# A smaller descriptor scratch, and one more place for weight chunks, in an mLSTM, convolution, attention and expert layer

## The chip, the cores and the metric

The kernel runs on one core of a Trainium2 chip. The metric is the device time of one execution in microseconds; of the kernel before there are three runs and one profiled execution.

## What is computed

One layer of an encoder over 512 tokens of width 1024, in float32. A mixer adds three gated branches (a bidirectional mLSTM with 4 heads, a depthwise convolution of width 31, an attention with 8 heads and low-rank queries and keys), projected by `w_out`, to the input. Then each of 16 experts picks its 64 best tokens and adds a SwiGLU layer of them:

```
x   = x + W_out( sum_b sigmoid(G_b xn) * Branch_b(xn) ),  xn = RMSNorm(x)
aff = softmax(RMSNorm(x) @ w_router);  gate, idx = top_k(aff.T, 64)
h   = silu(xg @ w_e_gate) * (xg @ w_e_up)          # xg: the picked tokens, 64 x 1024 per expert
x   = x + scatter_add(idx, (h @ w_e_down) * gate)  # w_e_*: 16 x 1024 x 1536, 302 MB in all
```

## The kernel before

**The mixer** runs first. Projections are done in three float32r products per pair of tiles (high and low halves, split by ScalarE and VectorE at L166 and L167). At its start stands a stage for the mLSTM's gates: `agr`, the gains of its norm (128 x 512 floats, 256 kB), is asked for by GpSimd (POOL) at L582, `gf` is copied from `gall` by VectorE at L585, ScalarE takes `ab` from it in three steps (L587 to L589), GpSimd fills `zero`, `bc` and `mr` with zeros (L593 to L597), and VectorE scans (L600, L606). The scans end in `mrh`, which TensorE needs at L671. `agr` is first read by the norm of the first head (L734). All these tiles lie where tiles of the attention lay, so that their first writers wait for the attention's last products (`poa`, L560).

**The output projection** `w_out` runs in four column blocks n of 256, each over four token tiles (`pso`, L177 to L179 called at L964 ff.). The weights of blocks 2 and 3 are loaded in four pieces each (`woraw`, two buffers, L820) and split into `wo`. The router is computed between.

**The experts** go in pairs. Their weights come in chunks of 128 x 3072 floats (12 kB in each partition, 1536 kB in all, L892). A pair has 24: eight for each expert's gate and up products (`pg`, `pu`, `pm`, L1145), eight for the down products of both (`pd`, L1217). SP issues all chunk loads. Places for chunks lie in four rings, opened as memory comes free: the first while `w_out` is running, the second when one of its weight tiles is closed, the third and fourth when the mixer's pools are closed. Two chunks are loaded ahead into tiles whose own use comes later, `work` and `acc`. Places are taken in turn (`SLOTS`); a chunk that has been used calls for the next load (`used`), unless it lay in one of those two tiles.

```
RINGS = (8, 2, 1, 1)
ORDER = (0, 1, 2, 3, 4, 5, 6, 8, 9, 10, 7, 11, 12, 13)
AHEAD = (2, 5, RINGS[0])
...
        if n + 2 < NQ:
            for k in range(0, KT, 2):
                load_wo(n + 2, k, 2)
            for c in range(AHEAD[n], AHEAD[n + 1]):
                load(ORDER[c])
...
    def used(n):
        del chunks[n]
        if n not in own and nload[0] < NCH:
            load(nload[0])
            nload[0] += 1
```

The order of instructions on an engine or queue is not quite that of the program: a planner may put a later one first when it expects the earlier one to wait. Pools are stacked from two sides of each partition's memory; 16 kB of it are kept as scratch for the descriptors of transfers that GpSimd issues.

Of the kernel before, what the change touches and what calls it, by code (L numbers as in the profile page):

```python
# [36 lines left out]
CH = 2 * FF  # L37
# [11 lines left out]
MAGIC = float(0x5F3759DF)  # L49
LN_AT = 4  # L50
WARM = 10
RINGS = (8, 2, 1, 1)


ORDER = (0, 1, 2, 3, 4, 5, 6, 8, 9, 10, 7, 11, 12, 13)
SLOTS = [r for r, n in enumerate(RINGS) for _ in range(n)]
AHEAD = (2, 5, RINGS[0])
CONSTS = (
# [28 lines left out]
def hybrid_mlstm_conv_mla_ec_encoder_kernel(  # L87
    ctx: ExitStack, tc: tile.TileContext, a: dict, out: bass.AP, dbg=None
):
    nc = tc.nc  # L90
    PE, V, A, G, SY = nc.tensor, nc.vector, nc.scalar, nc.gpsimd, nc.sync
# [487 lines left out]
    mrl = gk.tile([NR, S], F32R, name="mrl")  # L579
    cols = gk.tile([P, 2, NT, NR], F32, name="cols")  # L580
    agr = gk.tile([P, HA, P], F32, name="agr")
    G.dma_start(agr, a["a_norm_g"])  # L582
    w1 = pools.open("w1")
    gf = w1.tile([NR, S], F32, name="gf")
    V.tensor_copy(gf, gall[64 : 64 + NR, :])  # L585
# [270 lines left out]
    )  # L856
    rings = [pools.open("ring1", RINGS[0])]
    seq = [0]
# [22 lines left out]
    def load(n, place=None):  # L881
        c = place
        if c is None:
            c = rings[SLOTS[seq[0] % len(SLOTS)]].tile(
                [P, CH], F32, tag="chunk", name="chunk"
            )
            seq[0] += 1
        src = source(n)
        w = src.shape[1]
        step = CH // 3 if n == NCH - 1 else w  # L890
        for c0 in range(0, w, step):
            SY.dma_start(c[:, c0 : c0 + step], src[:, c0 : c0 + step])  # L892
        chunks[n] = c

    for n in range(AHEAD[0]):
        load(ORDER[n])
    wrg = rt.tile([P, KT, NE], F32, name="wrg")
# [63 lines left out]
    for n in range(NQ):  # L961
# [19 lines left out]
# [5 lines that stand above are left out]
        if n == NQ - 2:  # L986
            pools.close("wo0")
            rings.append(pools.open("ring2", RINGS[1]))
            for c in range(RINGS[0], RINGS[0] + RINGS[1]):
                load(ORDER[c])  # L990

# [8 lines left out]

    rings.append(pools.open("ring4", RINGS[3], side="right"))
    rings.insert(2, pools.open("ring3", RINGS[2], side="right"))
# [5 lines left out]
    work = ex2.tile([P, CH], F32, name="work")  # L1008
# [4 lines left out]


    accf = acc.rearrange("p t d -> p (t d)")
    own = {7: work, 13: accf[:, :CH]}
    for n in ORDER[RINGS[0] + RINGS[1] :]:
        load(n, own.get(n))
    nload = [len(ORDER)]

# [429 lines left out]
def _build(nc, arrays, dbg=None):  # L1450
    args = {
        k: nc.dram_tensor(
            f"in_{k}_dram", v.shape, mybir.dt.from_np(v.dtype), kind="ExternalInput"
        ).ap()
        for k, v in arrays.items()
    }
    out = nc.dram_tensor("out_0_dram", (S, D), F32, kind="ExternalOutput").ap()
    with tile.TileContext(nc) as tc:
        hybrid_mlstm_conv_mla_ec_encoder_kernel(
            tc, args, out, dbg(nc) if dbg else None  # L1460
        )
# [13 lines left out]
```

## Time and profile before

| | |
|---|---|
| median of 3 runs | 1282.27 us (1282.19 to 1282.41) |
| profiled execution | 1281.83 us |
| its span in the trace | 1280.1 us |
| mean granted TensorE clock | 0.995 |
| TensorE busy | 1233.7 us, 96% |
| VectorE, ScalarE, GpSimd busy | 596.9, 287.0, 23.7 us |
| moved by transfers | 351.05 MB, 274 GB/s on average |

The profiled execution is 1.73 us longer than its span, for what lies around it. Engines are PE (TensorE), PEld (its weight loads), DVE (VectorE), ACT (ScalarE), POOL (GpSimd) and SP; a q behind the name is the engine's sequencer or queue. The page cuts the span into 40 slices of 32 us.

### The profile page before, as it was taken

The page shows a single profiled execution, that of the slowest core. Times are in us where ns is not written, and L with a number is a line of the kernel's source. Part 1 is how long each engine was busy: PE and PEld are TensorE (multiplying, and loading weights), DVE is VectorE, ACT ScalarE, POOL GpSimd, SP SyncE. Part 2 cuts the span into 40 slices and gives each one's busy share as a digit, 9 for nine tenths or more (in the row PEclk, how much of TensorE's full clock was granted, in tenths as well). Part 3 has the DMA queues.
Part 4 walks back from the last instruction along what each step waited for, and adds up shares of the span by engine and source line. Part 5 has one row for each costly group of instructions (what it writes and reads, how often), then busy time and mean ns, then how long its engine had stood idle before and what let it go on. Part 6 is the DMA issues. An engine that isn't in the chain of part 4 may idle for free.

```text
span 1280.1 us, 15572 instructions
## 1 busy us (share of the span) xinstructions
PE 1233.7 (96%) x6224; PEld 735.6 (57%) x6224; DVE 596.9 (47%) x1438; ACT 287.0 (22%) x560; POOL 23.7 (2%) x56
## 2 busy tenths in 40 slices
PE   6999999999999999999999999999999999988997
PEld 6997777768878888994344353443433433423432
DVE  7379999999874655344321323213131231131122
ACT  5354444445333443221100000001000000010010
POOL 2000000001000000000000000000000000000000
PEclk9999999999999999999999999999999999999999
DMA  6231211112123244588999999999999999999996
GB/s 247 81 93 29 77 54 51 50 48 76 50 67 99 83 129 149 206 351 334 392 380 427 425 425 425 425 426 425 424 425 426 426 424 424 425 425 426 426 423 273
DMA packets 43496, 351.05 MB, mean 274 GB/s; under 512 B 4960, under 2 KB 5856, under 8 KB 18208
## 3 DMA queue, kind: packets, MB, share of 16 engines
q1 hardware_dynamic: 42768, 348.75, 67.7%
q8 instruction: 49, 0.80, 0.3%
q10 hardware_dynamic: 576, 1.05, 0.2%
q0 software_dynamic: 80, 0.26, 0.1%
q14 instruction: 23, 0.19, 0.0%
HBM read 347.94 MB, written 2.10 MB: 273 GB/s over the span
## 4 chain that ended last, share of the span: by engine, by line
PE 75%; DMA 19%; DVE 4%; ACT 1%; issue 1%; DVEq 0%; ACTq 0%; SPq 0%
DMA chunk<-in_w_gu_dram 9%; DMA chunk<-in_w_dn_dram 9%; PE pd L1217 8%; PE pg L1145 6%; PE pu L1145 6%; PE pm L1145 5%; PE psg L178 3%; PE psg L179 3%; PE psg L177 3%; PE px L1056 3%; PE psz L177 3%; PE psz L178 2%; PE psz L179 2%; PE psy L178 2%; PE psy L179 2%; PE psy L177 2%
## 5 line engine op out<-in xcount | busy, mean ns | idle before, releaser
L1217 PE MATMUL pd<-chunk,work 128*64 128x512 f32 x672 | 161.3, 607 | 5.7 <-DMA chunk<-in_w_dn_dram 5.7
L1145 PE MATMUL pg<-chunk,xg 128*64 128x512 f32 x504 | 148.3, 600 | 6.0 <-DMA chunk<-in_w_gu_dram 5.9
L1145 PE MATMUL pu<-chunk,xg 128*64 128x512 f32 x504 | 145.6, 593 | 0.0
L1145 PE MATMUL pm<-chunk,xg 128*64 128x512 f32 x504 | 137.8, 593 | 0.0
L1157 DVE SCALAR_TENSOR_TENSOR work<-pu,rsl,work 128x512 f32<-128x512 f32 x16 | 12.0, 751 | 211.0 <-PE pu L1145 211.0
L1217 PEld LDWEIGHTS pd<-chunk,work 128*64 128x64 f32 x672 | 48.3, 139 | 98.1 <-issue 88.1
L167 DVE TENSOR_TENSOR wlo<-wraw,whi 128x1024 fp32r<-128x1024 f32 x56 | 68.4, 1224 | 40.6 <-ACT whi L166 40.2
L167 DVE TENSOR_TENSOR yhl<-pd,yhl 128x512 fp32r<-128x512 f32 x18 | 12.4, 692 | 160.2 <-ACT yhl L166 160.2
L754 DVE SCALAR_TENSOR_TENSOR cacc<-upad,hwb,cacc 128x512 f32<-128x512 f32 x120 | 86.8, 743 | 0.1
L1156 ACT ACTIVATE work<-pg,rsl 128x512 f32<-128x512 f32 x16 | 11.0, 687 | 337.9 <-PE pg L1145 328.7
L166 ACT CAST whi<-wraw 128x1024 fp32r<-128x1024 f32 x56 | 58.8, 1052 | 112.7 <-PE psg L178 65.8
L1145 PEld LDWEIGHTS pu<-chunk,xg 128*64 128x64 f32 x504 | 40.1, 137 | 70.8 <-issue 70.8
L1145 PEld LDWEIGHTS pm<-chunk,xg 128*64 128x64 f32 x504 | 38.7, 137 | 71.6 <-issue 71.6
L177 PE MATMUL psg<-xh,whi 128*128 128x512 f32 x192 | 76.3, 397 | 2.5 <-ACT whi L166 2.5
L1145 PEld LDWEIGHTS pg<-chunk,xg 128*64 128x64 f32 x504 | 37.1, 136 | 72.0 <-issue 56.5
L178 PE MATMUL psg<-xl,whi 128*128 128x512 f32 x192 | 76.8, 400 | 0.0
L179 PE MATMUL psg<-xh,wlo 128*128 128x512 f32 x192 | 75.9, 395 | 0.0
L178 PE MATMUL psz<-xl,whi 128*128 128x512 f32 x160 | 64.7, 404 | 0.0
L179 PE MATMUL psz<-xh,wlo 128*128 128x512 f32 x160 | 64.6, 404 | 0.0
L177 PE MATMUL psz<-xh,whi 128*128 128x512 f32 x160 | 64.5, 403 | 0.0
L1036 DVE SCALAR_TENSOR_TENSOR yhl<-pb,affr,before 128x512 fp32r<-128x512 f32 x64 | 47.8, 746 | 31.1 <-PE pb L1033 31.1
L166 ACT CAST yhl<-pd 128x512 fp32r<-128x512 f32 x18 | 10.5, 586 | 217.0 <-PE pd L1217 192.4
(374 smaller groups left out, 2091.6 us busy)
## 6 DMA issues: line engine op xcount, KB each, us to landing
chunk<-in_w_gu_dram SPq DMA_DIRECT2D x118, 1536.0 KB, 26.5
chunk<-in_w_dn_dram SPq DMA_DIRECT2D x60, 1536.0 KB, 29.4
wraw<-in_w_z_dram SPq DMA_DIRECT2D x44, 512.0 KB, 3.5
chunk<-in_w_ga_dram SPq DMA_DIRECT2D x8, 1024.0 KB, 24.1
chunk<-in_w_dl_dram SPq DMA_DIRECT2D x3, 1536.0 KB, 23.9
mxt<-in_x_dram SPq DMA_DIRECT2D x8, 512.0 KB, 5.0
chunk<-in_w_gb_dram SPq DMA_DIRECT2D x2, 1536.0 KB, 21.6
nraw<-in_w_v_dram SPq DMA_DIRECT2D x2, 1024.0 KB, 5.4
```

The lines of the kernel that those rows point to most:

```text
L166: A.copy(hi, src)
L167: eng.tensor_sub(lo, src, hi.bitcast(F32))
L177: PE.matmul(ps, lh, rh, start=i == 0, stop=False)
L178: PE.matmul(ps, lh, rl, start=False, stop=False)
L179: PE.matmul(ps, ll, rh, start=False, stop=i == n - 1)
L754: V.scalar_tensor_tensor(cacc[:, i], u, w, cacc[:, i], op0=ALU.mult, op1=ALU.add)
L1036: V.scalar_tensor_tensor(rjunk, pb, aff[:, t, e : e + 1], before[:, (NT - 1 - t) * P : (NT - 1 - t) * P + S], op0=ALU.subtract, op1=ALU.is_gt,
L1056: PE.matmul(px[:, kk], x1[:, t, k * P : (k + 1) * P], flat[:, t], start=t == 0, stop=t == NT - 1,)
L1145: last = PE.matmul(ps[hf * 64 : hf * 64 + 64, :], xs, w[:, o : o + S], start=k == 0, stop=k == KT - 1,)
L1156: A.activation(hb[:, 0], pg, AF.Silu, scale=r)
L1157: V.scalar_tensor_tensor(hb[:, 0], pu, gr, hb[:, 0], op0=ALU.mult, op1=ALU.mult)
L1217: last = PE.matmul(pd[i * 64 : i * 64 + 64, :], hT[i][:, rt], chunks[ns[i]][:, r * S : (r + 1) * S], start=rt == 0, stop=rt == 11,)
```

## The change

The descriptor scratch is 1 kB instead of 16, and the first ring has nine places instead of eight. The chunks loaded ahead of the first use are fifteen instead of fourteen: chunk 11 comes ahead of chunk 7, and `acc` takes chunk 14 instead of 13. The transfer of `agr`, the only one that GpSimd issues, is issued by ScalarE.

```
-RINGS = (8, 2, 1, 1)
-ORDER = (0, 1, 2, 3, 4, 5, 6, 8, 9, 10, 7, 11, 12, 13)
+RINGS = (9, 2, 1, 1)
+ORDER = (0, 1, 2, 3, 4, 5, 6, 8, 9, 10, 11, 7, 12, 13, 14)
...
-    G.dma_start(agr, a["a_norm_g"])
+    A.dma_start(agr, a["a_norm_g"])
...
-    own = {7: work, 13: accf[:, :CH]}
+    own = {7: work, 14: accf[:, :CH]}
...
-    nc = _bacc.Bacc("TRN2", target_bir_lowering=False, num_devices=1)
+    nc = _bacc.Bacc("TRN2", target_bir_lowering=False, num_devices=1, dynamic_dma_scratch_size=1024)
```

## Rows read from the trace of the kernel before

**Rows 1.** The page: an engine's busy time, and transfer rate in 40 slices.

```profile
PE 1233.7 (96%) x6224; PEld 735.6 (57%) x6224; DVE 596.9 (47%) x1438; ACT 287.0 (22%) x560; POOL 23.7 (2%) x56
...
GB/s 247 81 93 29 77 54 51 50 48 76 50 67 99 83 129 149 206 351 334 392 380 427 425 425 425 425 426 425 424 425 426 426 424 424 425 425 426 426 423 273
```

**Rows 2.** Busy time by stretch; the last columns are granted clock, transfer share, GB/s.

```profile
595.00:680.00 85.00, 85.00 (x424) 34.67 (x422) 22.05 (x59) 6.89 (x11) 0.00 (x0) 1.00 0.95 386
...
680.00:760.00 80.00, 79.30 (x392) 32.91 (x390) 19.85 (x48) 5.24 (x9) 0.00 (x0) 1.00 1.01 425
```

**Rows 3.** The chain that ended last, 1040 to 1180 us (start, length, what).

```profile
1134.05 29.47 DMA chunk<-in_w_dn_dram
1163.57 5.36 PE pd L1217 x22
```

**Rows 4.** Waits of TensorE from 860 to 1170 us (total, times, longest).

```profile
PE pg L1145 <- DMA chunk<-in_w_gu_dram: 5.9, 7, 0.9
PE pd L1217 <- DMA chunk<-in_w_dn_dram: 5.7, 6, 2.0
```

**Rows 5.** Busy time by stretches of 5 us, columns as in rows 2.

```profile
555.00:560.00 5.00, 5.00 (x45) 5.00 (x45) 2.42 (x7) 1.29 (x4) 0.00 (x0) 1.00 0.30 104
575.00:580.00 5.00, 4.54 (x36) 3.91 (x34) 4.02 (x23) 1.86 (x7) 0.00 (x0) 1.00 0.27 111
...
665.00:670.00 5.00, 5.00 (x22) 2.31 (x24) 2.48 (x4) 0.00 (x0) 0.00 (x0) 1.00 0.64 270
```

**Rows 6.** SP's queue from 538 to 598 us (start, length, line, transfer, count).

```profile
539.92 1.83 SPq L820 DMA_DIRECT2D woraw<-in_w_out_dram  x2
541.81 0.43 SPq L892 DMA_DIRECT2D chunk<-in_w_gu_dram  x1
557.36 1.83 SPq L820 DMA_DIRECT2D woraw<-in_w_out_dram  x2
559.25 7.04 SPq L892 DMA_DIRECT2D chunk<-in_w_gu_dram  x4
579.58 0.33 SPq L892 DMA_DIRECT2D work<-in_w_gu_dram  x1
...
596.37 0.33 SPq L892 DMA_DIRECT2D chunk<-in_w_gu_dram  x1
```

**Rows 7.** What SP's queue waited for, 600 to 690 us.

```profile
SPq L892 <- PE pm L1145: 52.0, 15, 7.9
SPq L892 <- PE pd L1217: 27.7, 6, 10.9
```

**Rows 8.** Timeline of ScalarE, VectorE and GpSimd from 268 to 272 us.

```profile
268.28 1.09 ACT L655 ACTIVATE ao<-psz 128x512 f32<-128x512 f32 x2 [2.99 <-PE poa L560]
...
268.86 0.74 POOL L582 DMA_DIRECT2D agr<-in_a_norm_g_dram  x1 [217.54 <-PE poa L560]
269.01 2.35 DVE L585 COPY gf<-gall 36x512 f32<-36x512 f32 x1
...
270.53 0.55 POOL L597 MEMSET mr<- 36x512 f32 x1
...
271.39 0.63 ACT L587 ACTIVATE ab<-gf 36x512 f32<-36x512 f32 x1 [1.51 <-DVE gf L585]
```

**Rows 9.** Timeline of VectorE: the next operation on `gf`.

```profile
272.66 0.41 DVE L590 TENSOR_SCALAR gf<-gf 36x512 f32<-36x512 f32 x1
```

**Rows 10.** Line 1275, the output's transfers: ns shortest, median, longest.

```profile
L1275 ACTq DMA_DIRECT2D out_dram<-acc x4: 338/338/377, 1270.5 to 1276.8; - x4
```

**Rows 11.** Waits of TensorE from 250 to 595 us.

```profile
PE psg L177 <- ACT whi L166: 2.5, 1, 2.5
...
PE pr L671 <- ACT mrh L169: 0.5, 1, 0.5
```

**Rows 12.** Timeline: last split of `w_out`'s last block, and that block's first product.

```profile
564.73 0.69 DVE L167 TENSOR_TENSOR wo<-woraw,wo 128x512 fp32r<-128x512 f32 x1 [0.42 <-ACT wo L166]
...
567.02 0.36 PE L177 MATMUL pso<-wo,mgh 128*128 128x256 f32 x1
```

## The prediction

> **What bounds the kernel now.** I read the page first, then the busy time by stretch, the chain that ended last, the waits of TensorE and the order of SP's queue. The page shows TensorE busy nearly throughout and the transfer rate rising to 425 GB/s from the middle on [rows 1]. The question is which of the two sets the end. By stretch, the transfers run at 386 GB/s on average from 595 to 680 us and at 425 from 680 on [rows 2], and the page holds that rate until the last slice [rows 1]. So from about 680 us the stream of weight chunks has no gap left. The chain shows what the end hangs on: its last transfer is a w_dn chunk that lands at 1134.05 + 29.47 = 1163.5 us, and the down products start on it at once [rows 3]; what follows in the chain is TensorE's own work. Before that, TensorE waits for chunks 13 times, 5.9 + 5.7 = 11.6 us in all, between 860 and 1170 us [rows 4]. Hence the end is: the landing of that chunk, plus work that comes after it. A stream that is earlier by d moves the end by d, as long as d stays under those 11.6 us.
>
> What sets the stream's place in time? Before 680 us it has holes. Three carry the argument: 555 to 560 us at 104 GB/s, 575 to 580 us at 111, 665 to 670 us at 270 [rows 5]. Against 425 they are 5 x 321/425 = 3.8 us, 5 x 314/425 = 3.7 us and 5 x 155/425 = 1.8 us of idle transfer. The first two lie where SP has nothing it may issue: between the single chunk at 541.81 and the pair of w_out pieces at 557.36, and between the four chunks from 559.25 and `work` at 579.58 [rows 6]. The third is of another kind. From 600 to 690 us SP's loads wait for places: 52.0 us for `pm` and 27.7 us for `pd` products that still read the old chunk [rows 7]. The stream after the last hole is therefore anchored to TensorE: one load for each chunk that TensorE gives up, started when it gives it up.
>
> **The ring, part by part.** A chunk is 128 x 12 kB = 1.573 MB, at 425 GB/s [rows 2] 3.70 us. With the ninth place in the first ring fifteen chunks are asked for before TensorE uses any, instead of fourteen. The load that follows the use of chunk m is then one chunk further on in the weights than today, for every m from 14 on (from 0 to 12 as well; at m = 13 it is two, since the chunk held in `acc` is now 14 and not 13). TensorE gives places up at the same times, because until about 860 us it waits for no chunk. So each transfer slot behind the hole at 665 us carries the next chunk, and each chunk lands one slot, 3.70 us, earlier. The bytes are the same; what pays is that the extra chunk goes through in a hole.
>
> Where it goes through: its load stands among those of the stage that issues at 541.81 and 559.25 [rows 6]. Behind either it meets a hole of 3.8 or 3.7 us [rows 5], as long as itself. Should it be pushed behind 579.58, the holes between 595 and 680 us still take it: 85 x (425 - 386)/425 = 7.8 us of idle transfer [rows 2]. If none took it, it would cost nothing and bring nothing. Bounds: 0 and 3.70 us gained; I take 3.70, since a hole of that length stands beside either place in the queue.
>
> The new order (11 ahead of 7, 14 in `acc`) and the renumbered places issue nothing more. Chunk 7 goes to `work`, still at 579.58, behind TensorE's last `pso`; it lands some 7 us later and is the eighth to be used, while TensorE's first use is about 596 us, when the next load goes out [rows 6]. That cover is over 10 us, and if it were gone the cost would be one chunk, 3.70 us, in a stretch where the 11.6 us of later waits would take it up. The ninth place costs no wait that I can find: its ring opens on the side and at the height where only tiles of earlier branches have lain. The smaller scratch has no time of its own: after the change no transfer is issued from POOL.
>
> **The move of `agr`.** Today POOL issues it at 268.86 us for 0.74 us and then does its three memsets, the last ending at 270.53 + 0.55 = 271.08 [rows 8]. Over just that time VectorE's copy `gf` of 36 x 512 takes 2.35 us and ends at 271.36, 0.28 us behind the last memset [rows 8]; an operation on the same tile from SBUF to SBUF takes 0.41 [rows 9]. So the copy stands still while POOL works. Without the 0.74 us in front, the memsets can end 0.74 us earlier, and the copy with them. Behind it ScalarE has been idle 1.51 us for `gf` [rows 8], TensorE then waits 2.5 us for a cast that stands behind ScalarE's steps on it, and 0.5 us for `mrh`, the end of VectorE's scans [rows 11]. TensorE is short of work there, so I pass the 0.74 us on to the end in full. Bounds: nothing, if the copy is slow for a reason of its own, and 2.35 - 0.41 = 1.94 us, if the memsets leave the stretch too.
>
> The Trainium skill, page "SBUF — State Buffer", section "SBUF: two separate sides", states that VectorE and GpSimd share a pair of ports that the first to start holds for its whole instruction while the other waits. By that rule the 0.74 us is real and the sum is 4.44; this trace agrees, with the copy's end 0.28 us behind POOL's. The Trainium skill, page "DMA: Bandwidth & Descriptors", section "Issuing engines are not separate DMA queues", says that the choice of the issuing engine saves only the time to initiate the transfer, which speaks against a gain here. By that the sum is 3.70; no run yet shows it.
>
> ScalarE now holds the transfer. The nearest row is its issue of the output, 0.338 us [rows 10]. It must wait, as POOL did, until the attention's last products have ended; queued behind it are the `ao` activations, the casts of `oT` and the steps on `gf`. ScalarE was idle for the end of those same products, and idle again for the 1.51 us before `ab` [rows 8], so I take nothing. Without that cover it would be 0.34 us, by POOL's own row 0.74.
>
> **Sum.** Profiled execution: 1281.83 - 3.70 - 0.74 = 1277.39 us. It stands 0.44 under the median of the runs, so 1277.8 for the median. With both bounds of `agr`: 1282.27 - 3.70 - 1.94 = 1276.6, and 1282.27 - 3.70 + 0.34 = 1278.9.
>
> **Rivals.**
> Only the place pays: the copy `gf` is slow for itself, or the time won there is lost in planning. For it: that the copy waits is inferred from ends that follow one another, from one row. 1282.27 - 3.70 = 1278.6 us.
>
> The place is filled and nothing moves: the load ends up where the stream had no hole, or TensorE's work behind 1163.5 us turns out to be held by something other than the chunk. For it: TensorE is 96% busy [rows 1], so little slack is left. Against it: 11.6 us of waits for chunks in front of that point [rows 4]. Time: only `agr`, 1281.5 us.
>
> Slower: the extra load goes in front of w_out. The order of SP's queue is planned, and today one chunk already goes between the two pairs of w_out pieces [rows 6]. The last piece is split by 564.73 + 0.69 = 565.4 us, and the product that starts on w_out's last quarter runs from 567.02 [rows 12]; its later rows of weights leave some 3.5 us of slack. The second pair goes out when the first has been split. If n chunks came ahead of the first pair at 539.92, the pieces would be 3.70 n later: two give a stall of 7.4 - 3.5 = 3.9 us, under the gain of 4.4; three give 7.6 us, and the sum 1282.27 - 4.44 + 7.6 = 1285.4; four (all of that group) 11.3 us, 1289.1. It decides from three on. Against it: the kernel writes all loads behind the pieces.
>
> A larger gain: besides all this the memsets clear the copy's way, or TensorE's 2.5 us idle closes further: 1276 us or below.
>
> **How the numbers follow.** Place and `agr` together 0.57, the place alone 0.16, nothing moves 0.11, slower 0.10, larger gain 0.06. The likeliest gives 1277.8, in its own range 1276.6 to 1278.9. Upwards I reach to the case in which nothing moves: 1276.3 to 1281.9. A measurement here can tell about 0.2%, 2.56 us, from no change. The first, second and last case are faster by more than that, 0.79, of which I take off 0.02 for holes that are only partly filled: 0.77; within it 0.13; slower 0.10.
>
> **What would show it.** Right: four chunks from the group behind 541.81 instead of three; the hole at 555 or 575 us nearly gone; the hole at 665 us still there at the same length; TensorE's waits for chunks down from 11.6 to about 8 us; `gf` at some 1.6 us and ending near 270.6. Wrong: a `pso` product that waits for `wo`, ScalarE held in front of 268.28 us, a hole at 665 us that has grown by a chunk, or waits for chunks that have not shrunk.

## The result, and the profile after

The changed kernel takes 1276.03 us (median of 6 runs, 1275.37 to 1279.43), the kernel before 1282.34 in the same set (6 runs, 1282.19 to 1285.32): the ratio is 0.995, with a 95% interval of 0.994 to 0.9961. It is 6.3 us faster. The forecast was 1277.8, and its range began at 1276.3, so the time fell 0.27 us below the range: the direction was right and the gain too small.

The profiled execution of this set is the slowest of its six, 1279.43 us with a span of 1277.7. A second set of runs of the same kernel (experiment e0 below) has its median, 1275.82, as its profiled execution, with a span of 1274.1. Both are read here.

The page of the first, TensorE's line, to [rows 1]:

```profile
PE 1230.5 (96%) x6224; PEld 734.1 (57%) x6224; DVE 596.2 (47%) x1438; ACT 287.1 (22%) x560; POOL 23.2 (2%) x55
```

Busy time by stretch of the changed kernel, to [rows 2, 5] and with their columns:

```profile
595.00:680.00 85.00, 85.00 (x421) 35.24 (x418) 20.81 (x52) 6.90 (x11) 0.00 (x0) 1.00 0.96 388
665.00:670.00 5.00, 5.00 (x26) 1.65 (x24) 0.80 (x2) 0.00 (x0) 0.00 (x0) 1.00 0.70 256
680.00:760.00 80.00, 79.30 (x392) 32.21 (x391) 19.46 (x47) 5.24 (x9) 0.00 (x0) 1.00 1.01 426
```

SP's queue of the changed kernel up to 600 us, to [rows 6]:

```profile
539.46 0.42 SPq L892 DMA_DIRECT2D chunk<-in_w_gu_dram  x1
555.02 1.83 SPq L820 DMA_DIRECT2D woraw<-in_w_out_dram  x2
556.90 7.04 SPq L892 DMA_DIRECT2D chunk<-in_w_gu_dram  x5
577.22 0.33 SPq L892 DMA_DIRECT2D work<-in_w_gu_dram  x1
...
594.01 0.33 SPq L892 DMA_DIRECT2D chunk<-in_w_gu_dram  x1
596.59 2.90 SPq L892 DMA_DIRECT2D chunk<-in_w_dn_dram  x2
```

The extra chunk stands in the second group, which has five chunks instead of four. Since the mixer ends 2.4 us earlier here, the two holes ahead of 595 us stand some 2.4 us earlier too. Busy time in stretches of 10 us around each of them, first in the kernel before, then in the changed one:

```profile
552.40:562.40 10.00, 10.00 (x89) 10.00 (x88) 3.79 (x14) 3.98 (x12) 0.00 (x0) 1.00 0.60 212
574.60:584.60 10.00, 9.48 (x62) 7.89 (x61) 7.65 (x44) 3.10 (x11) 0.00 (x0) 1.00 0.57 214
```

```profile
550.00:560.00 10.00, 10.00 (x88) 10.00 (x88) 3.80 (x14) 3.87 (x12) 0.00 (x0) 1.00 0.62 226
572.20:582.20 10.00, 9.48 (x63) 7.93 (x61) 7.65 (x44) 3.11 (x11) 0.00 (x0) 1.00 0.91 354
```

The first hole is as empty as before. The second carries (354 - 214) x 10 = 1.40 MB more (1.55 in e0, with 369 GB/s), against 1.573 MB of a chunk: that is where the extra chunk went through. The hole at 665 us is still there. At 594 us one chunk of `w_gu` is left to ask for instead of two, and then `w_dn` begins: each load behind TensorE's use of a chunk now brings the next one.

Timeline of ScalarE's queue, VectorE and GpSimd in the changed kernel, to [rows 8]:

```profile
266.60 0.39 ACTq L582 DMA_DIRECT2D agr<-in_a_norm_g_dram  x1
266.68 0.52 POOL L593 MEMSET zero<- 36x512 f32 x1 [214.97 <-PE poa L560]
267.14 0.52 POOL L595 MEMSET bc<- 36x512 f32 x1
267.32 0.62 DVE L585 COPY gf<-gall 36x512 f32<-36x512 f32 x1
267.61 0.81 POOL L597 MEMSET mr<- 36x512 f32 x1
268.01 0.62 ACT L587 ACTIVATE ab<-gf 36x512 f32<-36x512 f32 x1
```

The copy `gf` takes 0.62 us instead of 2.35 and no longer stands behind the last memset: it ends at 267.94, 0.28 us behind the second, and the third, with 0.81 instead of 0.55 us, is the one that gets longer. What follows in TensorE (its waits from 250 to 595 us, to [rows 11]):

```profile
PE pr L671 <- ACT mrh L169: 1.2, 1, 1.2
...
PE pc L616 <- DVE al L604: 1.1, 1, 1.1
```

The single wait of 2.5 us is gone, and so is the short one of 0.5; two of 1.2 and 1.1 stand in their place. In the kernel before, TensorE's clock fell behind that wait. Its busy time by stretches of 1 us shows it in the granted clock, the third column from the end:

```profile
278.00:279.00 1.00, 1.00 (x4) 0.81 (x3) 0.99 (x2) 0.99 (x2) 0.00 (x0) 0.50 0.00 0
279.00:280.00 1.00, 1.00 (x3) 0.80 (x3) 0.97 (x2) 1.00 (x2) 0.00 (x0) 0.50 0.00 0
280.00:281.00 1.00, 1.00 (x4) 0.74 (x3) 1.00 (x2) 0.29 (x1) 0.00 (x0) 0.50 0.00 0
```

At 0.50 (1.2 GHz) eight products follow one another every 0.43 us from 277.50 on, where the same products stand 0.23 us apart at 2.4 GHz: that is 8 x 0.2 = 1.6 us lost. In the changed kernel the clock is 1.00 throughout that stretch.

The end of the chain, to [rows 3], in the first profile and in that of e0:

```profile
1130.07 29.47 DMA chunk<-in_w_dn_dram
1159.58 7.06 PE pd L1217 x22
```

```profile
1128.10 29.48 DMA chunk<-in_w_dn_dram
1157.62 5.36 PE pd L1217 x22
```

The chunk lands at 1157.58 us in e0, 5.9 earlier than before. In the first profile it lands 2.0 us later than in e0, and the 22 products behind it take 7.06 us instead of 5.36, since the clock falls behind the wait for that chunk (0.83 from 1160 to 1170 us). These two things are its 3.6 us over e0, and the same program gave both. In e0 the clock falls as well, but one chunk earlier (0.85 from 1150 to 1160 us): the products there end later, and the wait for the last chunk is 0.6 us instead of 2.0. TensorE's waits for chunks, from 850 to 1180 us, in the two, to [rows 4]:

```profile
PE pd L1217 <- DMA chunk<-in_w_dn_dram: 6.3, 5, 2.0
PE pg L1145 <- DMA chunk<-in_w_gu_dram: 6.0, 7, 0.9
```

```profile
PE pg L1145 <- DMA chunk<-in_w_gu_dram: 6.1, 8, 0.9
...
PE pd L1217 <- DMA chunk<-in_w_dn_dram: 2.9, 4, 1.0
```

### The profile page after: what moved, and what is told of

The parts are those of the page before. It is cut to its first block, busy times and chain, and to the rows that moved or that the text cites. A ratio compares the mean times of both kernels' runs of the same rounds, so it can differ in the third digit from the quotient of the medians.

```text
span 1277.7 us, 15571 instructions
## 1 busy us (share of the span) xinstructions
PE 1230.5 (96%) x6224; PEld 734.1 (57%) x6224; DVE 596.2 (47%) x1438; ACT 287.1 (22%) x560; POOL 23.2 (2%) x55
## 4 chain that ended last, share of the span: by engine, by line
PE 82%; DMA 12%; DVE 4%; ACT 1%; issue 1%; SPq 0%; DVEq 0%; ACTq 0%
PE pd L1217 11%; DMA chunk<-in_w_dn_dram 7%; PE pg L1145 7%; PE pu L1145 6%; PE pm L1145 6%; DMA chunk<-in_w_gu_dram 5%; PE px L1056 4%; PE psg L179 3%; PE psg L177 3%; PE psg L178 3%; PE psz L178 3%; PE psz L179 3%; PE psz L177 3%; PE pxs L1271 2%; PE psy L177 2%; PE psy L178 2%
```

## The experiments

The kernel before was timed beside each set: 1283.35 us for e0 to e3, 1282.73 for e4 to e7, 1283.56 for e8 and e9, one run of 1282.79 for e10 and e11. The table splits each profiled execution at the mixer's end, taken as the start of the last `pso` product; the rest runs from there to the end of the span. No experiment leaves any of the computation out.

| | median us (range) | ratio, 95% interval | profiled | mixer's end | rest |
|---|---|---|---|---|---|
| before | 1282.34 | | 1281.83 | 579.27 | 700.8 |
| after | 1276.03 (1275.37 to 1279.43) | 0.995 (0.994 to 0.9961) | 1279.43 | 576.91 | 700.8 |
| e0 | 1275.82 (1275.34 to 1276.77) | 0.9941 (0.9929 to 0.9953) | 1275.82 | 576.85 | 697.3 |
| e1 | 1288.70 (1288.11 to 1288.82) | 1.0039 (1.0026 to 1.0052) | 1288.82 | 584.62 | 702.5 |
| e2 | 1279.33 (1278.95 to 1281.36) | 0.997 (0.9959 to 0.9981) | 1279.33 | 576.28 | 701.3 |
| e3 | 1277.97 (1276.83 to 1279.05) | 0.9956 (0.9944 to 0.9968) | 1276.84 | 577.98 | 697.1 |
| e4 | 1276.05 (1275.11 to 1276.88) | 0.9948 (0.9936 to 0.996) | 1276.88 | 576.31 | 698.9 |
| e5 | 1279.42 (1278.99 to 1281.46) | 0.9975 (0.9967 to 0.9984) | 1281.46 | 576.37 | 703.3 |
| e6 | 1289.38 (1286.33 to 1292.00) | 1.0054 (1.0041 to 1.0067) | 1286.37 | 579.76 | 704.9 |
| e7 | 1280.45 (1280.19 to 1281.73) | 0.9983 (0.9975 to 0.9992) | 1280.35 | 577.82 | 700.8 |
| e8 | 1275.68 (1274.82 to 1277.95) | 0.9946 (0.9934 to 0.9959) | 1274.82 | 575.93 | 697.2 |
| e9 | 1280.41 (1279.76 to 1281.98) | 0.998 (0.997 to 0.9989) | 1280.64 | 578.10 | 700.8 |
| e10 | one run | | 1280.64 | 578.00 | 700.9 |
| e11 | one run | | 1281.21 | 577.36 | 702.1 |

The rest varies from run to run by some 3.5 us with the waits for chunks, as the two profiles of the changed kernel show; where it matters, the medians decide.

**e0, the changed kernel again**, as the measure for e1 to e3.

> The changed kernel once more, for a second profile. Theory (place plus mixer): two terms add up. The mixer ends about 2.3 us earlier (seen in the first profile of the change), and the ninth place moves the chunk stream by one chunk, 3.7 us: 6.0 us under the kernel before, near 1276.3, and the profiled execution that was only 2.4 us faster is one in which TensorE ran at half clock for some 3 us behind its last wait for a chunk. Rival (mixer only): the place gives nothing, the median lies near 1280 and the faster runs are those without a fall of the clock; then the stream of chunks in this profile stands no more than 2.3 us ahead of that of before.

It confirms the first set: 1275.82. Against the profiled execution of before, 1281.83 - 1275.82 = 6.0 us; 2.4 of it lie ahead of the mixer's end and 3.6 behind. Against the median of before in its own set the gain is 1283.35 - 1275.82 = 7.5 us, where the first set gave 6.3.

**e1, the move of `agr` alone**, in the kernel before.

```
-    G.dma_start(agr, a["a_norm_g"])
+    A.dma_start(agr, a["a_norm_g"])
```

> The kernel before with agr issued by ScalarE and nothing else. Prediction on record: 0.74 us faster (1281.6). Theory (the copy gf and the clock): gf falls from 2.35 to about 0.6 us, TensorE's wait of 2.5 us behind it shrinks under the length after which its clock fell, and the mixer ends some 2 us earlier: about 1280. Rival (memory and plan): the 2.3 us of the change come from another order of the mixer that the larger room brings, and this kernel gains 0.7 us or less.

It is slower, though the copy takes 0.62 us here too. The planner, with ScalarE's issue to reckon with, writes another order: `pc` comes ahead of the gates' products. TensorE's waits from 250 to 595 us and its busy time by stretch show the price:

```profile
PE pc L616 <- DVE al L604: 4.0, 1, 4.0
```

```profile
270.00:280.00 10.00, 6.03 (x29) 4.70 (x27) 9.96 (x15) 9.84 (x14) 0.41 (x1) 0.95 0.06 23
280.00:290.00 10.00, 10.00 (x25) 6.36 (x25) 8.11 (x10) 4.49 (x10) 1.38 (x2) 0.50 0.16 52
290.00:300.00 10.00, 10.00 (x47) 8.32 (x46) 6.78 (x20) 2.50 (x6) 1.73 (x8) 0.87 0.17 53
```

After 4.0 us without work TensorE runs at half its clock from the wait's end to beyond 290 us; the mixer ends 5.35 us later than before. The order alone is not the price: e6 below has TensorE's order of e1 in the mixer and the same wait of 4.0 us, but its clock is low for a shorter time:

```profile
280.00:290.00 10.00, 10.00 (x39) 6.90 (x38) 9.28 (x15) 5.75 (x12) 3.10 (x8) 0.86 0.26 75
290.00:300.00 10.00, 10.00 (x59) 8.68 (x58) 9.68 (x29) 3.09 (x6) 0.00 (x0) 1.00 0.12 36
```

Its mixer ends only 0.5 us later than that of before. So an edit can free a copy and lose by the wait that the new order brings, and most of the loss is in how long the clock stays low behind it; why it stays low longer in e1 is not shown.

**e2, the change without the ninth place**: scratch 1 kB and `agr` on ScalarE, but `RINGS = (8, 2, 1, 1)` and 14 chunks ahead, as before. TensorE's order in the mixer is that of the changed kernel.

> Scratch of 1 kB and agr on ScalarE as in the change, but eight places and fourteen chunks ahead. Its mixer has the order of instructions of the changed kernel. Theory (place plus mixer): 2.3 us under before, about 1280.0, and 3.7 us over the changed kernel. Rival (mixer only): as fast as the changed kernel.

1279.33 against 1275.82 in the same set: the ninth place is worth 3.5 us. The smaller scratch with `agr` on ScalarE is worth 4.0 against the kernel before in this set. (SP's queue differs too: two of the fourteen chunks go out at 388 and 391 us already, and the group at 556 us has two instead of four.)

**e3, the change with `agr` still on GpSimd, in front of the memsets** (scratch 4 kB, since GpSimd then still needs some).

```
-    A.dma_start(agr, a["a_norm_g"])
+    G.dma_start(agr, a["a_norm_g"])
...
-    dynamic_dma_scratch_size=1024
+    dynamic_dma_scratch_size=4096
```

> The change with agr still issued by GpSimd, over a scratch of 4 kB: the ninth place without the move of agr. Theory (place plus mixer): the place's 3.7 us and none of agr's, about 1278.6, with gf still over 2 us long. If instead most of the mixer's gain comes from the room that the smaller scratch leaves, it is as fast as the changed kernel, about 1276.3. Rival (mixer only): within 1 us of before.

1277.97, 2.15 us slower than e0 by the medians (the two profiled executions are 1.0 apart). The copy is held as before (timeline of VectorE and GpSimd):

```profile
267.02 0.74 POOL L582 DMA_DIRECT2D agr<-in_a_norm_g_dram  x1 [215.51 <-PE poa L560]
267.18 2.35 DVE L585 COPY gf<-gall 36x512 f32<-36x512 f32 x1
...
268.69 0.55 POOL L597 MEMSET mr<- 36x512 f32 x1
```

Yet its mixer ends 1.3 us earlier than that of before: with more room the planner writes another order (e2 and e0 have one order on TensorE with eight and nine places, so it isn't the place that changes it), TensorE's 2.5 us of idle time come in two parts (2.0 and 0.4), and the granted clock stays at 1.00.

**e4 and e5, when the ninth place is filled.** Both are e2 with the ninth place in a pool of its own, held by one small copy and then filled once ahead of a pair of experts: the first pair (e4, about 591 us) or the third (e5, about 760 us).

```
+        if p == 0:            # e5: p == 2
+            held = ringx.tile([P, CH], F32, tag="chunk", name="chunk")
+            V.tensor_copy(held[:, 0:1], xg[:, 0, 0:1])
+            turn.insert(0, 4)
+            load(nload[0])
+            nload[0] += 1
```

> Eight places in the first ring and a ninth of its own, same room as in the change; fourteen chunks are loaded ahead, and the ninth place is first filled when the first chunk is used (a copy of one element of xg into it keeps it busy until about 592 us). Theory (the holes): the holes between 595 and 680 us, 7.8 us of idle transfer, still take the extra chunk, so it is as fast as the changed kernel, about 1276.3. Rival (only what is loaded ahead of the first use counts): 3.7 us slower than the changed kernel, about 1280.

> As e4_fill_first_use, but the ninth place is first filled when the third pair of experts begins, about 760 us, when the stream of chunks has had no hole for 80 us. Theory (the holes): the same thirteen places in the ring bring nothing any more, 3.7 us slower than the changed kernel and as fast as the one with eight places, about 1280. Rival (the depth of the ring counts): as fast as the changed kernel, about 1276.3.

e4 is as fast as the changed kernel (1276.05), e5 no faster than eight places (1279.42 against 1279.33). Their busy time by stretch, e4 first:

```profile
540.00:595.00 55.00, 52.87 (x386) 43.34 (x386) 29.58 (x133) 12.66 (x43) 0.00 (x0) 1.00 0.85 343
595.00:680.00 85.00, 85.00 (x422) 35.24 (x420) 21.41 (x53) 6.89 (x11) 0.00 (x0) 1.00 0.98 404
```

```profile
540.00:595.00 55.00, 52.86 (x386) 43.34 (x386) 29.54 (x132) 12.71 (x43) 0.00 (x0) 1.00 0.82 332
595.00:680.00 85.00, 85.00 (x422) 35.25 (x420) 21.35 (x53) 6.89 (x11) 0.00 (x0) 1.00 0.96 392
```

Up to 680 us e4 moves 55 x (343 - 332) + 85 x (404 - 392) = 1.6 MB more, one chunk, with the same mixer; from 680 us on both run at 425 GB/s. A deeper ring alone, once the stream has no gaps, brings nothing here. What pays is the chunk that goes through in a gap.

**e6, seven places**: e1 with `RINGS = (7, 2, 1, 1)` and 13 chunks ahead.

> agr on ScalarE over the full scratch, and a first ring of seven places with thirteen chunks ahead: one place less than in e1_agr_alone. Theory (the holes): one chunk, 3.7 us, slower than e1_agr_alone. Rival (the place gives nothing): as fast as e1_agr_alone.

1289.38, scattered over 5.7 us, and only 0.7 above e1, since its mixer ends 4.9 us earlier than e1's in the profiles. From there to the end it takes 704.9 us, against 702.5 in e1 and 700.8 in the kernel before. The scatter goes in part with the clock: its two runs at a mean granted clock of 0.994 took 1286.3 and 1286.4 us, one at 0.997 took 1288.4, and the three at 0.989 to 0.992 took 1290.3 to 1292.0, where e1's five, at 0.988 to 0.991, took 1288.1 to 1288.8. The sign fits a place's worth; with such scatter the size does not follow from this run.

**e7, the kernel before with `agr` issued by GpSimd behind its memsets.** TensorE's order is that of before, product by product.

```
-    G.dma_start(agr, a["a_norm_g"])
...
     G.memset(mr, 0.0)
+    G.dma_start(agr, a["a_norm_g"])
```

> The kernel before with agr still issued by GpSimd, but behind the three memsets and not ahead of them. As the prediction had it, the copy gf waits for all of GpSimd's work in its way, so it ends 0.3 us behind the last memset, 0.74 us earlier than before, and lasts about 1.6 us. Rival (the descriptors): it is GpSimd's making of the transfer's descriptors that holds VectorE and not the memsets; gf lasts about 0.6 us, and a later operation of VectorE from SBUF to SBUF is held up instead, by some 2 us.

1280.45, 2.3 us faster by one line moved. `gf` takes 0.62 us with the memsets around it. TensorE's waits for `whi`, `al` and `mrh` are 0.8, 1.0 and 0.8 us, and the clock doesn't fall.

**e8, the change with `agr` on GpSimd behind the memsets** (e3 with the line of e7).

> The change with one difference: agr stays on GpSimd, but is issued behind its three memsets instead of in front of them (scratch 4 kB, so that GpSimd can issue it). Against the run with agr in front (1277.97, 0.9956) only the place of that one issue differs. Theory (what holds the copy gf is GpSimd's transfer issue in front of it, not the memsets; the changed kernel owes its last two us to the copy being free): gf takes about 0.62 us amid the memsets, and the time is that of the changed kernel, 1275.8 to 1276.1. Rival 1 (what counts is that ScalarE issues it, or the order of TensorE's work that goes with that): the time stays at 1278. Rival 2 (the memsets hold the copy, as the prediction had it): gf about 1.6 us, 0.7 us earlier than with agr in front, 1277.2.

1275.68, as e0 (1275.82) and 2.3 us faster than e3, both of another set. TensorE's order in the mixer is that of e3. `gf` takes 0.62 us. So it isn't ScalarE that pays, but that nothing is issued in front.

**e9, the kernel before with `agr` issued by SP.** The order of TensorE, VectorE and ScalarE is that of before.

> The kernel before with agr issued by SP instead of GpSimd, at the same point; scratch, ring and the order of TensorE's, VectorE's and ScalarE's work are those of before. GpSimd then does its memsets with no transfer in front of them. Theory (GpSimd's issue holds the copy): gf about 0.62 us, TensorE's 2.5 us without work near 275 us shrinks to under 1.5 and its granted clock does not fall behind it; 1280.4, as with the issue behind the memsets. Rival (the memsets hold it): gf about 1.6 us, ends 0.74 earlier, 1281.6. Rival 2 (agr off GpSimd is slower in the old room whatever the order, as when ScalarE alone took it): 1286 or more. SP's loads behind agr wait for the end of the attention with it; should that delay weights that are used next, the time goes up and the trace shows TensorE waiting for whi at a later place.

1280.41, as e7, `gf` 0.62 us.

**e10 and e11, what holds the copy**: in e10 the issue stays in front, but VectorE fills `bc` and `mr`, so that one memset is left behind it; in e11 the issue stands between the first memset and the other two.

```
-    G.memset(bc, 0.0)         # e10
+    V.memset(bc, 0.0)
...
-    G.memset(mr, 0.0)
+    V.memset(mr, 0.0)
...
     G.memset(zero, 0.0)       # e11; the line at L582 is gone
+    G.dma_start(agr, a["a_norm_g"])
```

> The kernel before, agr issued in front by GpSimd as there, but bc and mr are filled by VectorE, so that only one of GpSimd's memsets (zero) stands behind the issue. In the kernel before gf ends 0.28 us behind the last of three memsets and takes 2.35 us. Theory A (the copy that arrives during the issue waits until GpSimd has done all that it has queued behind it): gf ends 0.28 us behind the one memset that is left, 0.74 + 0.54 + 0.28 - 0.15 = about 1.4 us long. Theory B (the issue itself holds it, whatever stands behind): 2.35 us as before. Theory C (the prediction's, it waits for the memsets one by one): also 1.4, so A and C are told apart by the other run of this pair, not by this one. The whole time says little, since VectorE has two more fills of some 0.3 us to do.

> The kernel before with GpSimd's issue of agr between its first memset (zero) and the other two; TensorE's order is that of before. The copy gf is then ready some 0.15 us into the issue or just ahead of it. Theory A (an issue that is under way or next lets the copy wait until GpSimd's run of work is over): gf ends 0.28 us behind the last memset, some 1.8 to 2.3 us long, and the time stays at that of before, 1282 to 1283. Theory D (the copy goes in behind whatever GpSimd instruction runs when it comes, as it did behind bc where no issue stood in front): gf ends at most 0.3 us behind the issue, about 1.0 us or less, and the time is 1280 to 1281.

Timelines of VectorE and GpSimd, e10 and then e11:

```profile
269.34 0.73 POOL L582 DMA_DIRECT2D agr<-in_a_norm_g_dram  x1 [217.59 <-PE poa L560]
269.49 0.81 DVE L585 COPY gf<-gall 36x512 f32<-36x512 f32 x1
270.08 0.68 POOL L593 MEMSET zero<- 36x512 f32 x1
```

```profile
268.33 0.52 POOL L592 MEMSET zero<- 36x512 f32 x1 [217.13 <-PE poa L560]
268.98 0.42 DVE L584 COPY gf<-gall 36x512 f32<-36x512 f32 x1
269.19 0.74 POOL L593 DMA_DIRECT2D agr<-in_a_norm_g_dram  x1 [0.33 <-issue]
```

In e10 the copy ends 0.23 us behind the issue, and the memset behind it gets longer (0.68 instead of 0.54). That is neither of the two lengths expected, 1.4 and 2.35: the issue alone holds the copy to its end only. In e11 it runs ahead of the issue. Both are faster than the run of before beside them, 1280.64 and 1281.21 against 1282.79, with one run each; TensorE's order is that of before in e11, and another one in e10.

## Why the prediction missed

**What bounds the kernel, and the ring's term: right.** The end hangs on the stream, and the stream on the holes ahead of 680 us; e4 against e5 shows it, with the same ring and only the time of filling changed. The term was 3.70 us; measured are 3.5 (e2 to e0) and 3.4 (e5 to e4), and 3.6 behind the mixer's end in the profiles of before and e0 (none in the first profile of the change, the slowest of its runs). The extra load went behind the second pair of w_out pieces, one of the two places named, and through the second hole; the first was left as it was. No `pso` waited for `wo`, so that the slower rival had no ground. The waits for chunks shrank from 11.6 to 9.0 us in e0, about as forecast; in the slowest run, 12.3, they had not.

**The term of `agr` failed.** The step was: "So the copy stands still while POOL works. Without the 0.74 us in front, the memsets can end 0.74 us earlier, and the copy with them." It took the three memsets for what held the copy, and gave it 1.6 us. But the copy takes 0.62 us amid the same memsets (after, e1, e7, e8, e9), and 0.81 with the issue and one memset (e10). Only the issue followed by three memsets gives 2.35 us (before, e3). The bound 1.94 us of that step was nearly met by the copy, 2.35 - 0.62 = 1.73, though under the condition "if the memsets leave the stretch too", which they didn't.

The Trainium skill, page "SBUF — State Buffer", section "SBUF: two separate sides", says that of a GpSimd operation and a VectorE operation that uses the shared ports, the one that starts first holds them for its whole length and the other waits. The rows agree in part: in the changed kernel the copy ended 0.28 us behind the second memset, and the third memset took 0.81 us. They don't show what let three memsets in a row go ahead of the waiting copy in the kernel before. The Trainium skill, page "DMA: Bandwidth & Descriptors", section "Issuing engines are not separate DMA queues", names only the sequencer's time to start a transfer as what can be saved by issuing from several engines. Here e3 to e0 is 2.15 us; e3 to e8, where GpSimd still issues, is as much, so the gain is that of the copy beside the issue and not of the transfer.

**What the stall is worth was mis-sized too.** The prediction passed the copy's 0.74 us on one to one. The runs give 2.15 (e3 to e0, one set), 2.3 (e3 to e8, two sets) and 2.3 (before to e7, TensorE's order unchanged). Where it comes from, the profiles of before and e7 show. The attention's last products start at

```profile
264.60 3.65 PE L560 MATMUL poa<-pT,vn 128*64 128x512 f32 x14
```

```profile
264.97 3.65 PE L560 MATMUL poa<-pT,vn 128*64 128x512 f32 x14
```

and from there to the mixer's end it is 579.27 - 264.60 = 314.67 us before and 577.82 - 264.97 = 312.85 in e7, 1.8 less. TensorE's idle time at the gates falls by only 0.4 (2.5 + 0.5 to 0.8 + 1.0 + 0.8). The remaining 1.4 is close to the 1.6 us that the half rate cost before; it is a remainder and not measured by itself. The prediction didn't look at the clock in that stretch. The other 0.5 of the median's 2.3 is within the scatter of single runs.

**The smaller scratch was not free of effect.** "The smaller scratch has no time of its own" is true of the scratch, but its room changes the planner's order: with the copy held as before, the mixer of e3 ends 1.3 us earlier, and the same move of `agr` to ScalarE costs 5.35 us in the old room (before to e1) and gains 2.15 in the new one (e3 to e0). This was not among the steps, and another order can also lose, as e1 shows. No run has the smaller scratch alone. In the profiles the order and the copy don't simply add up: the mixer's end moves by 1.3 us with the order alone (e3), by 1.45 with the copy alone (e7), and with both by 2.4 (e0) and 3.3 (e8). One fall of the clock, taken away by either, would explain this: in each of the four the clock stays at 1.00, which is 1.6 us, and TensorE's idle time at the gates is 3.0 us in before and in e3 (2.0 + 0.4 + 0.6), 2.6 in e7, 2.3 in e0 (1.2 + 1.1) and 1.5 in e8 (1.0 + 0.5). By this estimate from the rows e3, e7, e0 and e8 gain 1.6, 2.0, 2.3 and 3.1 us.

**ScalarE's issue at nothing: not contradicted.** It took 0.39 us there, and e8, which issues from GpSimd, is within 0.14 us of e0. What e1 lost is not the issue's time but the wait, and the clock behind it, that came with the order written around it.

So the forecast's 3.70 + 0.74 stands against 3.6 (place) + 2.4 (mixer) between the profiled executions of before and e0, and against 3.5 + 4.0 by the medians of e0's set. Both are splits of one measured difference, not independent sums. The rival "a larger gain" named 1276 us or below, "the memsets clear the copy's way, or TensorE's 2.5 us idle closes further": its time was met within 0.03 us (1276.03, and 1275.82 in e0), by the copy getting its way beside the memsets, the clock holding, and an order of the planner that the rival didn't name. It had a chance of 0.06, because 1.6 us for the copy was held for the likelier reading of a single row.

**What stays open**: why a copy that comes during the issue loses to three memsets in a row and not to one. And why the first profile's chunk landed 2.0 us later than in e0, with the same order of work.

## What to carry to other kernels

An extra place for loads paid one load's time here when it was filled while the stream still had gaps, and nothing when it was filled later: look for the gap, not for the depth. When a short operation of VectorE is several times as long as its like, look at what GpSimd does at its start and try the issue behind the fills first; that was one moved line and 2.3 us here. And where a planner orders the work, read the order again after each edit, of memory too, and read the granted clock behind each wait of TensorE that an edit makes longer or shorter.

## What was not expected of the hardware

- A VectorE copy of 36 x 512 float32 from SBUF to SBUF took 2.35 us beside GpSimd's issue of a transfer (0.74 us) followed by three memsets of the same size, 0.81 us beside the issue and one memset, 0.62 amid three memsets alone, and 0.42 behind one memset, with nothing running on GpSimd when it began (e11).
- TensorE's clock was granted at half behind waits of 2.46 us (before) and 4.0 us (e1), for some 3.4 us in the one and beyond 290 us, over 10 us, in the other, though TensorE was busy all through it; in e6, with the order and the wait of e1, for some 3.4. Behind the mixer's waits of 0.8 to 1.2 us (e7, e0) and one of 2.0 us (e3) it stayed at 1.00. Yet in e0 it fell to half near 1150 us, where the waits from 850 us on are 1.0 us or less each.
- The same program, in its two profiles, ran the 22 products behind its last awaited chunk in 5.36 and in 7.06 us, by the clock behind that wait.
